# Sums and split of s4, two sums of s3 and four residual sums on VectorE instead of GpSimd

## The chip, the cores and the metric

The kernel runs on one core of a Trainium2 chip. A core has a matrix engine (PE in the profile), a vector engine (DVE), a scalar engine (ACT), a general engine (POOL, called GpSimd in the code) and a queue engine that starts transfers (SP). The metric is the device time of one execution in microseconds (us).

## The reference, cut to what matters

The kernel computes one layer of an encoder on 1024 tokens of width 1024, all in float32. Three sub-layers follow one another; each is normed ahead and behind, and added to x.

```python
def _rms_norm(x, gain):
    return x * lax.rsqrt(jnp.mean(x * x, axis=-1, keepdims=True) + RMS_EPS) * gain
def _swiglu(x, w_in, w_out):                    # w_in: 1024 x 5632, w_out: 2816 x 1024
    g, u = jnp.split(x @ w_in, 2, axis=-1)
    return (jax.nn.silu(g) * u) @ w_out
...
h = _swiglu(_rms_norm(x, ffn1_pre_norm), ffn1_w_in, ffn1_w_out)          # FFN1
x = x + 0.5 * _rms_norm(h, ffn1_post_norm)
m = _token_mixing(_rms_norm(x, mix_pre_norm), w_mix_in, ..., w_mix_out)  # mix
x = x + _rms_norm(m, mix_post_norm)
h = _swiglu(_rms_norm(x, ffn2_pre_norm), ffn2_w_in, ffn2_w_out)          # FFN2
x = x + 0.5 * _rms_norm(h, ffn2_post_norm)
```

`_token_mixing` projects to 6656 columns (`u @ w_mix_in`), runs retention and neighbourhood attention on them, and ends with the product with `w_mix_out`.

## The kernel before, in words

**Products.** PE multiplies float32 numbers as sums of shorter ones. Each operand is split in a high part and a low part: `Core.split` lets ACT cast the high part (L61) and another engine subtract it from the source to get the low part (L62). That engine is DVE unless the caller names one in `eng`. A product is then three matmuls, high with high (L88), high with low and low with high (L89, L90). A weight arrives by DMA as `wraw` and is split into `wh` and `wl` just before its use, 512 columns at a time; in the out-projection of the mix the moving operand `graw` is split in the same way into `gh` and `gl`.

**Winograd factors.** The products with the layer's input X (FFN1 and FFN2, and most of the mix's projection) use one level of the Strassen-Winograd scheme, with seven products in place of eight. `Winograd.put` makes X's seven factors, each with a high and a low half: a11, a12, a22 and the sums s1 to s4. X comes in eight token tiles of 128. For tiles 0 to 3 a call only splits a11 or a12. For tiles 4 to 7, the second half of X, a first call (g = 0) copies the transposed tile to a temporary (`cmb`, L278) and begins s3 from it (L282, L283). A second call (g = 1) splits a22 and makes s1 (L288), s2 (L290) and s4 (L293, L294); each of s1 to s4 has a split of its own (`s1h`/`s1l`, ..., `s4h`/`s4l`). `put` returns the split of s4, which the caller runs a little later. All these instructions work on 128x512 elements.

**The two transitions.** Between FFN1 and the mix (683 to 732 us in the profile), and between the mix and FFN2 (1603 to 1667 us), the tokens of one sub-layer become the factors of the next. `Core.flip` transposes a token tile on PE into the bank `pt` (L127) and calls `put` on it. In the second transition `Ep.__call__` does the end of a token first: squares and their sums on ACT (L220), `rstd` on POOL (L98, for the root of 128 numbers), the scaled row on DVE (L227), the residual sum (L229), squares again (L231), `rstd` again, and the scaled row for the next sub-layer (L118). In the kernel before, POOL makes L293, L294 and the low half of s4 for tiles 4 to 7 in both transitions; L282 and L283 for tiles 4 and 5 in the second one (`wx.s3_on_pool = (4, 5)`); and L229 for tiles 6 and 7.

**What sets the order.** Each engine works through its own list of instructions, one after the other, and waits at an instruction until what it needs is there. The lists are not in the order of the source: the framework's scheduler builds them from the whole program with a model of costs, and a change of an instruction's engine can move others. To fill PE during a transition the first products of the next sub-layer that need only a11 and a12 run between the flips. `Pairs` and `leads` do this: each begins the products of a weight tile into banks, which are finished, or added up by DVE (L509 to L535), when the other factors are there. POOL also issues the stores (L68), SP the loads.

Of the kernel before, what the change touches and what calls it, by code (L numbers as in the profile page):

```python
# [13 lines left out]
ALU = mybir.AluOpType  # L14
# [24 lines left out]
class Core:  # L39
# [6 lines left out]
    def __init__(self, tc, const, wpool, psum, dram):  # L46
        self.tc, self.nc = tc, tc.nc
        self.const, self.wpool, self.psum, self.dram = const, wpool, psum, dram
        nc = self.nc
        self.ident = const.tile([P, P], F32, name="ident")  # L50
        make_identity(nc, self.ident)
        self.mhalf = const.tile([P, 8], F32, name="mhalf")
        nc.gpsimd.memset(self.mhalf, -0.5)
        self.small = None
# [46 lines left out]
    def norm_T(self, x, gain, t, pool, put, ss=None):  # L101

        nc = self.nc
        xn = pool.tile([P, D], F32, tag="tmp", name="tmp", bufs=3)
        if ss is None:
            ss = self.small.tile([P, 3], F32, tag="ss3", name="ss3", bufs=6)
            for b in range(2):  # L110
                bs = slice(b * 512, (b + 1) * 512)
                nc.scalar.activation(xn[:, bs], x[:, bs], AF.Square, scale=1.0 / 32.0, accum_out=ss[:, b:b + 1])
        with self.tc.high_priority(offset=100):
            nc.vector.tensor_scalar(ss[:, 2:3], ss[:, 0:1], ss[:, 1:2], EPS, ALU.add, ALU.add)
            r = self.rstd(ss[:, 2:3], 1)
        for b in range(2):
            bs = slice(b * 512, (b + 1) * 512)
            nc.vector.scalar_tensor_tensor(xn[:, bs], x[:, bs], r[:, 0:1], gain[:, bs], op0=ALU.mult, op1=ALU.mult)  # L118

        return lambda: self.flip([xn[:, :512], xn[:, 512:]], t, put)  # L120

    def flip(self, halves, t, put, tag="pt", bufs=2):

        for g, h in enumerate(halves):
            pt = self.bank(tag, bufs)
            for j in range(4):
                self.nc.tensor.transpose(pt[:, j * P:(j + 1) * P], h[:, j * P:(j + 1) * P], self.ident)  # L127
            f = put(t, g, pt.rearrange("p (k t) -> p k t", k=4))
        return f
# [41 lines left out]
class Filler:  # L171
# [13 lines left out]
    def __call__(self, n):  # L185
        for _ in range(n):
            if not self.step():
                return
# [10 lines left out]
class Ep:  # L199
# [12 lines left out]
    def __call__(self, t, banks):  # L212
        c, nc = self.c, self.c.nc
        y = self.pool.tile([P, D], F32, tag="tmp", name="tmp", bufs=3)
        x = self.pool.tile([P, D], F32, tag="epx", name="epx", bufs=2)
        nc.sync.dma_start(x, self.resid(t))
        ss = c.small.tile([P, 3], F32, tag="ss3", name="ss3", bufs=6)
        f = 4.0 if self.half else 1.0
        for b in range(2):
            nc.scalar.activation(y[:, b * 512:(b + 1) * 512], banks[b], AF.Square,  # L220
                                 scale=(1.0 / 16.0 if self.half else 1.0 / 32.0), accum_out=ss[:, b:b + 1])
        nc.vector.tensor_scalar(ss[:, 2:3], ss[:, 0:1], ss[:, 1:2], f * EPS, ALU.add, ALU.add)
        r = c.rstd(ss[:, 2:3], 1)
        sx = c.small.tile([P, 3], F32, tag="ss3", name="ss3", bufs=6)
        for b in range(2):
            bs = slice(b * 512, (b + 1) * 512)
            nc.vector.scalar_tensor_tensor(y[:, bs], banks[b], r[:, 0:1], self.post[:, bs],  # L227
                                           op0=ALU.mult, op1=ALU.mult)
            (nc.gpsimd if t > 5 else nc.vector).tensor_tensor(x[:, bs], y[:, bs], x[:, bs], ALU.add)  # L229
            if self.pre is not None:  # L230
                nc.scalar.activation(y[:, bs], x[:, bs], AF.Square, scale=1.0 / 32.0, accum_out=sx[:, b:b + 1])  # L231
        (nc.sync.dma_start if self.pre is None else c.store)(self.dst(t), x)
        if self.pre is not None:
            return c.norm_T(x, self.pre, t, self.pool, self.put, sx)


class Winograd:
# [5 lines left out]

    def __init__(self, c, pools, tmp, bufs, spill=None, order=None):

        self.c, self.tmp, self.spill, self.s3_on_pool = c, tmp, spill, ()
        self.ops = {}
        if order is not None:
            for n in order:
                self.ops[n] = [pools.tile([P, 4, 512], F32R, name=f"{n}{q}") for q in "hl"]  # L250
            return
        self.pools, self.bufs = dict(zip(self.NAMES, (pools[i] for i in (0, 0, 1, 2, 2, 2, 2)))), bufs
# [10 lines left out]
    def put(self, t, g, pt):  # L263
        c, nc = self.c, self.c.nc
        ts = slice((t % 4) * P, (t % 4 + 1) * P)
        if t < 4:
            c.split(*self.part(("a11", "a12")[g], ts), pt)
            return

        def tmp():  # L270
            return self.tmp.tile([P, 4, P], F32, tag="cmb", name="cmb", bufs=4)

        h1, l1 = [q.bitcast(F32) for q in self.part("a11", ts)]
        h2, l2 = [q.bitcast(F32) for q in self.part("a12", ts)]

        if g == 0:
            self.a21, self.s3 = tmp(), tmp()
            nc.scalar.copy(self.a21, pt)  # L278
            if self.spill is not None:
                c.store(self.spill[:, :, ts], self.a21)  # L280
            eng = nc.gpsimd if t in self.s3_on_pool else nc.vector
            eng.tensor_tensor(self.s3, h1, self.a21, ALU.subtract)  # L282
            eng.tensor_tensor(self.s3, self.s3, l1, ALU.add)  # L283
            return
        a21, s3 = self.a21, self.s3
        s1 = a21 if self.spill is None else tmp()
        c.split(*self.part("a22", ts), pt)
        nc.vector.tensor_tensor(s1, pt, a21, ALU.add)  # L288
        c.split(*self.part("s3", ts), s3)
        nc.vector.tensor_tensor(s3, pt, s3, ALU.subtract)  # L290
        c.split(*self.part("s1", ts), s1)
        c.split(*self.part("s2", ts), s3)
        nc.gpsimd.tensor_tensor(s3, h2, s3, ALU.subtract)  # L293
        nc.gpsimd.tensor_tensor(s3, s3, l2, ALU.add)  # L294
        return lambda: c.split(*self.part("s4", ts), s3, eng=nc.gpsimd)


def first_factors(c, wx, pool, gpool, halves, sums, small, x, xt, gain, amid):
# [900 lines left out]
def trunk_layer(ctx: ExitStack, tc, x, xt, g1a, w1i, w1o, g1b, gma, wmt, wnv, wrv, logits, dtab, rope, bias,  # L1199
                wro, wno, wmo, gmb, g2a, w2i, w2o, g2b, out):  # L1200
    nc = tc.nc
# [5 lines left out]
    c = Core(tc, const, wpool, psum, dram)  # L1207
# [27 lines left out]
    wx = Winograd(c, apool, early, None, order=("s4", "a22", "s3", "a12", "s1", "s2", "a11"))  # L1235
# [23 lines left out]
    wx = Winograd(c, (x0pool, x1pool, spool), None, (4, 4, 2, 8, 8, 8, 8), d["a21"])  # L1259
# [224 lines left out]
    apool = pool(a_stack, "a2", "right")  # L1484
    cmb = pool(left, "cmb2")
    wx = Winograd(c, apool, cmb, None, order=("s4", "a22", "s1", "s3", "a12", "s2", "a11"))
    wx.s3_on_pool = (4, 5)
    with tc.tile_pool(name="ep2", bufs=1, reuse_waits="tile") as ep:
        rest = c.out_proj(KT, stream(c, gs, lambda k: d["m"][k]), lambda k: c.load_w(wmo[k]),
                          Ep(c, ep, gmb, g2a, False, rows(x1), rows(x2), wx.put))  # L1490
# [102 lines left out]
```

## Time and profile before

| | before |
|---|---|
| median of 3 runs | 2280.56 us (2280.09 to 2283.82) |
| profiled execution | 2281.11 us, span of its instructions 2279.3 us |
| busy share of the span | PE 97%, DVE 73%, ACT 44%, POOL 28% |
| first transition, 683 to 732 us | PE busy 40.4 of 49.0 us, DVE 43.6, ACT 23.7, POOL 24.7 |
| second transition, 1602.8 to 1667 us | PE busy 51.2 of 64.2 us, DVE 58.6, ACT 34.9, POOL 35.8 |

The profile comes from one execution. Its rows give the start of an instruction in us from the start of the span, its duration, engine, line, output and inputs; a mark such as `[1.79 <-DVE tmp L118]` says that the engine had been idle for 1.79 us and that DVE's instruction at L118 ended the wait. An instruction's duration overlaps the next one's start on its engine by a little, so the work of an engine is counted by starts. PE's clock can be lowered by the chip; the profile shows the clock that was granted as a share of full speed.

### The profile page before, as it was taken

Reading aid. Unit: us, or ns where it says so; the run is one execution under the profiler, and the core shown is the slowest. Engines: PE = TensorE matmul, PEld = TensorE weight load, DVE = VectorE, ACT = ScalarE, POOL = GpSimd, SP = SyncE. Lnnn points to the kernel's source line nnn. Section 1 sums busy time; section 2 is a strip of 40 time slices with the busy share of each in tenths; the row PEclk is TensorE's granted clock in tenths of the full one; section 3 lists DMA queues with packets and bytes.
Section 4 is the critical chain, followed back from the end, with each engine's and each line's share of the span. In section 5 each row is a group of like instructions: output and inputs, shape, how many; then the busy total and the mean of one; then the engine's idle time right before and its main releaser. Section 6 shows DMA issues by size and latency. Waiting matters only on the chain. (4 is left out here: it accounts for less than half of the span.)

```text
span 2279.3 us, 30175 instructions
## 1 busy us (share of the span) xinstructions
PE 2209.3 (97%) x10232; PEld 1830.4 (80%) x10232; DVE 1662.9 (73%) x2928; ACT 1000.5 (44%) x2086; POOL 629.9 (28%) x779
## 2 busy tenths in 40 slices
PE   7899999999998999999999999999899999999998
PEld 5678888888786887878888888887678888888886
DVE  7898878755568657769876678537988787876444
ACT  5444434332344222349875665315644343433232
POOL 1121212168424122301101222101522121115942
PEclk9999999999999999999999999999999999999999
DMA  6354434598654564557745566866535444449865
GB/s 249 134 184 145 175 130 175 197 378 293 201 178 157 176 184 128 150 174 256 218 165 165 166 217 235 292 215 208 169 134 177 161 156 158 143 146 368 304 225 181
DMA packets 152650, 448.31 MB, mean 197 GB/s; under 512 B 19312, under 2 KB 47088, under 8 KB 150384
## 3 DMA queue, kind: packets, MB, share of 16 engines
q1 hardware_dynamic: 111216, 314.23, 41.1%
q0 software_dynamic: 41280, 132.15, 16.0%
q8 instruction: 81, 1.33, 0.2%
q14 instruction: 73, 0.60, 0.1%
HBM read 305.80 MB, written 144.70 MB: 198 GB/s over the span
## 5 line engine op out<-in xcount | busy, mean ns | idle before, releaser
L62 DVE TENSOR_TENSOR wl<-wraw,wh 128x512 fp32r<-128x512 f32 x512 | 353.3, 708 | 85.4 <-ACT wh L61 84.7
L61 ACT CAST wh<-wraw 128x512 fp32r<-128x512 f32 x516 | 297.6, 618 | 192.1 <-PE ps L89 63.2
L88 PE MATMUL ps<-wh,g 128*128 128x512 f32 x484 | 188.6, 390 | 0.0
L89 PE MATMUL ps<-wl,g 128*128 128x512 f32 x484 | 188.5, 390 | 0.0
L90 PE MATMUL ps<-wh,g 128*128 128x512 f32 x484 | 188.4, 389 | 0.0
L552 ACT ACTIVATE c<-c 128x512 f32<-128x512 f32 x88 | 55.5, 632 | 204.3 <-DVE c L517 103.9
L62 DVE TENSOR_TENSOR wl<-w,wh 128x512 fp32r<-128x512 f32 x77 | 76.4, 1005 | 84.2 <-ACT wh L61 83.2
L62 DVE TENSOR_TENSOR wl<-x,wh 128x512 fp32r<-128x512 f32 x77 | 78.8, 1040 | 76.5 <-ACT wh L61 75.1
L88 PE MATMUL ps<-a11h,wh 128*128 128x512 f32 x276 | 111.6, 404 | 9.2 <-ACT wh L61 9.2
L61 ACT CAST wh<-t 128x512 fp32r<-128x512 f32 x58 | 36.0, 621 | 184.2 <-DVE t L511 184.2
L90 PE MATMUL ps<-a11h,wl 128*128 128x512 f32 x276 | 109.4, 397 | 2.6 <-DVE wl L62 2.4
L88 PE MATMUL ps<-a22h,wh 128*128 128x512 f32 x280 | 109.8, 392 | 0.0
L90 PE MATMUL ps<-a22h,wl 128*128 128x512 f32 x280 | 109.2, 390 | 0.6 <-DVE wl L62 0.6
L89 PE MATMUL ps<-a11l,wh 128*128 128x512 f32 x276 | 109.5, 397 | 0.1
L89 PE MATMUL ps<-a22l,wh 128*128 128x512 f32 x280 | 109.1, 390 | 0.0
L88 PE MATMUL ps<-a12h,wh 128*128 128x512 f32 x276 | 108.8, 394 | 0.3 <-ACT wh L61 0.3
L90 PE MATMUL ps<-a12h,wl 128*128 128x512 f32 x276 | 107.5, 390 | 0.0
L89 PE MATMUL ps<-a12l,wh 128*128 128x512 f32 x276 | 107.5, 389 | 0.0
L89 PEld LDWEIGHTS ps<-wl,g 128*128 128x128 f32 x484 | 90.9, 188 | 19.1 <-DVE wl L62 0.5
L90 PEld LDWEIGHTS ps<-wh,g 128*128 128x128 f32 x484 | 90.8, 188 | 19.0
L88 PEld LDWEIGHTS ps<-wh,g 128*128 128x128 f32 x484 | 90.9, 188 | 18.7
L88 PE MATMUL ps<-s2h,wh 128*128 128x512 f32 x232 | 91.8, 396 | 6.8 <-ACT wh L61 6.8
(433 smaller groups left out, 6443.8 us busy)
## 6 DMA issues: line engine op xcount, KB each, us to landing
wraw<-in_dram SPq DMA_DIRECT2D x218, 512.0 KB, 4.5
g<-g0s SPq DMA_DIRECT2D x44, 512.0 KB, 4.2
g<-g1s SPq DMA_DIRECT2D x44, 512.0 KB, 4.6
g<-g0a SPq DMA_DIRECT2D x33, 512.0 KB, 3.3
g<-g1a SPq DMA_DIRECT2D x33, 512.0 KB, 4.4
g0s<-gth POOLq DMA_DIRECT2D x44, 256.0 KB, 5.2
g0s<-cmb POOLq DMA_DIRECT2D x44, 256.0 KB, 3.7
g1s<-gth POOLq DMA_DIRECT2D x44, 256.0 KB, 4.9
```

What stands on the lines that cost most here:

```text
L61: self.done = [nc.scalar.copy(h, src).ins, (eng or nc.vector).tensor_tensor(l, src, hf, ALU.subtract).ins]
L62: (eng or nc.vector).tensor_tensor(l, src, hf, ALU.subtract).ins]
L88: mm(ps, a[0], b[0], start=start, stop=False)
L89: mm(ps, a[0], b[1], start=False, stop=False)
L90: mm(ps, a[1], b[0], start=False, stop=stop)
L552: nc.scalar.activation(gate[j], gate[j], AF.Silu)
```

## The change

All work of the second halves of X goes to DVE, and the three places that name POOL are gone: L293, L294 and the split of s4 (8 instructions of each, four tokens in each of two transitions), L282 and L283 for tiles 4 and 5 in the second transition (2 of each), and the residual sum L229 for tiles 6 and 7 (4). These are 32 instructions on 128x512 elements: 12 in the first transition and 20 in the second. What is computed stays the same. The rest of POOL's work (`rstd`, the issue of stores, the sums inside the FFNs) stays where it is.

```diff
@@ Ep.__call__
-            (nc.gpsimd if t > 5 else nc.vector).tensor_tensor(x[:, bs], y[:, bs], x[:, bs], ALU.add)
+            nc.vector.tensor_tensor(x[:, bs], y[:, bs], x[:, bs], ALU.add)
@@ Winograd.__init__
-        self.c, self.tmp, self.spill, self.s3_on_pool = c, tmp, spill, ()
+        self.c, self.tmp, self.spill = c, tmp, spill
@@ Winograd.put
-            eng = nc.gpsimd if t in self.s3_on_pool else nc.vector
-            eng.tensor_tensor(self.s3, h1, self.a21, ALU.subtract)
-            eng.tensor_tensor(self.s3, self.s3, l1, ALU.add)
+            nc.vector.tensor_tensor(self.s3, h1, self.a21, ALU.subtract)
+            nc.vector.tensor_tensor(self.s3, self.s3, l1, ALU.add)
...
-        nc.gpsimd.tensor_tensor(s3, h2, s3, ALU.subtract)
-        nc.gpsimd.tensor_tensor(s3, s3, l2, ALU.add)
-        return lambda: c.split(*self.part("s4", ts), s3, eng=nc.gpsimd)
+        nc.vector.tensor_tensor(s3, h2, s3, ALU.subtract)
+        nc.vector.tensor_tensor(s3, s3, l2, ALU.add)
+        return lambda: c.split(*self.part("s4", ts), s3)
@@ trunk_layer, second transition
-    wx.s3_on_pool = (4, 5)
```

One line fewer stands in `put`, so that L282, L283, L288 and L290 of the kernel before are L281, L282, L287 and L289 of the changed one, and its L293 and L294 become L292 and L293. The scheduler also builds other lists. Three places matter. The numbers behind the names tell tiles apart.

The first place is DVE's list in the first transition around the sums of token tile 7 (`cmb_6031`; `cmb_5946` is token tile 6). `wl_6071`, `wl_6088`, `wl_6107` and `wl_6124` are low halves of weights for the first products of the mix's projection. Before:

```order
L62 TENSOR_TENSOR s3l_5811<-cmb_5946,s3h_5810 128x4x128
L62 TENSOR_TENSOR wl_6071<-wraw_6067,wh_6070 128x512
L290 TENSOR_TENSOR cmb_5946<-pt_5951,cmb_5946 128x512
L62 TENSOR_TENSOR s1l_5816<-cmb_5956,s1h_5815 128x4x128
L62 TENSOR_TENSOR wl_6088<-wraw_6067,wh_6087 128x512
L62 TENSOR_TENSOR s2l_5820<-cmb_5946,s2h_5819 128x4x128
L62 TENSOR_TENSOR wl_6107<-wraw_6103,wh_6106 128x512
L62 TENSOR_TENSOR wl_6124<-wraw_6103,wh_6123 128x512
L282 TENSOR_TENSOR cmb_6031<-a11h_5217,cmb_6030 128x512
```

and with the change:

```order
L282 TENSOR_TENSOR cmb_6031<-cmb_6031,a11l_5218 128x512
L293 TENSOR_TENSOR cmb_5946<-cmb_5946,a12l_5227 128x512
L62 TENSOR_TENSOR a22l_5806<-pt_6036,a22h_5805 128x4x128
L287 TENSOR_TENSOR cmb_6041<-pt_6036,cmb_6030 128x512
L62 TENSOR_TENSOR s4l_5832<-cmb_5946,s4h_5831 128x4x128
L62 TENSOR_TENSOR s3l_5811<-cmb_6031,s3h_5810 128x4x128
L62 TENSOR_TENSOR s1l_5816<-cmb_6041,s1h_5815 128x4x128
L289 TENSOR_TENSOR cmb_6031<-pt_6036,cmb_6031 128x512
L62 TENSOR_TENSOR wl_6071<-wraw_6067,wh_6070 128x512
L62 TENSOR_TENSOR wl_6088<-wraw_6067,wh_6087 128x512
```

The low halves of these weights stood among token 6's instructions, and now they stand behind token 7's, while PE's list still has their products behind the transposes of token 7.

The second place is the end of the second transition on ACT. `s4h_14806` is the high half of s4 (of token 6 from `cmb_15951`, of token 7 from `cmb_16022`), and `wh_16156` is the weight of the first product with s3. The bracket names the engine or queue whose event a row waits for. Before:

```order
L61 CAST s3h_14812<-cmb_16022 128x4x128 [waits DVE_49]
L61 CAST s4h_14806<-cmb_15951 128x4x128 [waits Pool_49]
L61 CAST s1h_14810<-cmb_16021 128x4x128 [waits DVE_49]
L61 CAST s2h_14816<-cmb_16022 128x4x128 [waits DVE_49]
L552 ACT_TABLE_LOAD
L552 ACTIVATE c0_16123<-c0_16123 128x512 [waits DVE_49]
L61 CAST s4h_14806<-cmb_16022 128x4x128 [waits Pool_49]
L61 CAST wh_16156<-wraw_16128 128x512 [waits DMAHW6_49,DVE_49]
```

and with the change:

```order
L61 CAST s1h_14810<-cmb_16021 128x4x128 [waits DVE_49]
L61 CAST s4h_14806<-cmb_15951 128x4x128 [waits DVE_49]
L508 COPY gt_16353<-ps_16083 128x512 [waits PE_49,Activation_49]
L61 CAST s2h_14816<-cmb_16022 128x4x128 [waits DVE_49]
L61 CAST wh_16135<-t2_16130 128x512 [waits DVE_49]
L61 CAST s4h_14806<-cmb_16022 128x4x128 [waits DVE_49]
L551 ACT_TABLE_LOAD
L551 ACTIVATE c0_16123<-c0_16123 128x512 [waits DVE_49]
L61 CAST wh_16156<-wraw_16128 128x512 [waits DMAHW6_49,DVE_49]
```

Both casts of s4 now wait for DVE, and `wh_16156` still stands behind the last of them.

The third place is DVE's list in the second transition around `wl_16102`, the low half of a weight for the early products of FFN2 (`epx_15846` and `rstd_15864` belong to token 6's row for the next sub-layer, `cmb_15951` to token 6's sums and `cmb_16022` to token 7's). Before:

```order
L62 TENSOR_TENSOR wl_16064<-wraw_16043,wh_16063 128x512
L62 TENSOR_TENSOR wl_16085<-wraw_16081,wh_16084 128x512
L114 TENSOR_SCALAR ss3_15854<-ss3_15854 128x1
L62 TENSOR_TENSOR wl_16102<-wraw_16081,wh_16101 128x512
L118 SCALAR_TENSOR_TENSOR tmp_15862<-epx_15846,rstd_15864,gpre_14825 128x512 x2
```

and with the change:

```order
L62 TENSOR_TENSOR s1l_14811<-cmb_16021,s1h_14810 128x4x128
L289 TENSOR_TENSOR cmb_16022<-pt_16026,cmb_16022 128x512
L62 TENSOR_TENSOR s4l_14807<-cmb_15951,s4h_14806 128x4x128
L62 TENSOR_TENSOR wl_16102<-wraw_16081,wh_16101 128x512
L62 TENSOR_TENSOR s2l_14817<-cmb_16022,s2h_14816 128x4x128
```

It stood ahead of the rows and sums of the last two tokens, and now follows most of them.

SP's list changes in one place: the four loads of `tab` (the table for the rotary positions, L1344) stand ahead of two loads of `wraw` that they followed.

## The prediction

> **What bounds the kernel now.** I read the page first, for the busy shares, then the busy times of the two stretches that the change touches, and then PE's waits in each. In the windows the columns are length, PE, PEld, DVE, ACT and POOL busy, and the granted clock.
>
> ```profile
> PE 2209.3 (97%) x10232; PEld 1830.4 (80%) x10232; DVE 1662.9 (73%) x2928; ACT 1000.5 (44%) x2086; POOL 629.9 (28%) x779
> ```
> ```profile
> 1602.80:1667.00 64.20, 51.24 (x205) 37.82 (x204) 58.59 (x81) 34.86 (x74) 35.83 (x28) 0.92 0.36 120
> 683.00:732.00 49.00, 40.35 (x179) 31.87 (x177) 43.60 (x59) 23.65 (x44) 24.74 (x22) 0.96 0.49 160
> ```
> ```profile
> PE ps L89 <- DVE wl L62: 4.8, 3, 3.1
> PE pt L127 <- DVE tmp L118: 2.4, 2, 1.8
> PE ps L88 <- ACT wh L61: 1.8, 1, 1.8
> ```
> ```profile
> PE ps L88 <- ACT wh L61: 4.5, 1, 4.5
> PE ps L88 <- DVE ev L520: 3.0, 1, 3.0
> PE pt L127 <- DVE cmb L290: 1.5, 2, 1.2
> ```
>
> Over the whole span PE bounds the time. In the second transition PE is idle for 13 of 64.2 us and DVE for 5.6: there DVE sets the end, and PE waits mostly for its results (the first three waits). In the first transition (the last three) the 4.5 us wait is for a weight's arrival and is ahead of all that moves; the others hang on DVE.
>
> **What DVE's time consists of.** Two of the groups that move, as POOL does them, over the whole span (busy, mean ns, idle before and its cause):
>
> ```profile
> L62 POOL TENSOR_TENSOR s4l<-cmb,s4h 128x512 fp32r<-128x512 f32 x8 | 10.9, 1367 | 4.5 <-ACT s4h L61 4.4
> L229 POOL TENSOR_TENSOR epx<-tmp,epx 128x512 f32<-128x512 f32 x4 | 6.0, 1509 | 1.8 <-DVE tmp L227 1.8
> ```
>
> And what DVE does beside it, by group in the second transition, with ACT's casts of s4 there:
>
> ```profile
> L62 DVE TENSOR_TENSOR wl<-wraw,wh 128x512 fp32r<-128x512 f32 x22 | 19.3, 914 | 1.9 <-ACT wh L61 1.7
> L62 DVE TENSOR_TENSOR gl<-graw,gh 128x256 fp32r<-128x256 f32 x5 | 5.3, 1067 | 0.0
> L62 DVE TENSOR_TENSOR s1l<-cmb,s1h 128x512 fp32r<-128x512 f32 x4 | 3.9, 975 | 1.8 <-ACT s1h L61 1.8
> L229 DVE TENSOR_TENSOR epx<-tmp,epx 128x512 f32<-128x512 f32 x2 | 2.8, 1458 | 0.0
> L282 DVE TENSOR_TENSOR cmb<-a11h,cmb 128x512 f32<-128x512 f32 x2 | 2.0, 1006 | 0.0
> L283 DVE TENSOR_TENSOR cmb<-cmb,a11l 128x512 f32<-128x512 f32 x2 | 1.9, 934 | 0.0
> L530 DVE TENSOR_TENSOR wraw<-wraw,t 128x512 f32<-128x512 f32 x1 | 1.8, 1775 | 0.0
> ```
> ```profile
> L61 ACT CAST s4h<-cmb 128x512 fp32r<-128x512 f32 x4 | 2.5, 620 | 11.9 <-POOL cmb L294 11.9
> ```
>
> The single rows show why the means differ. The first fence is POOL's timeline, the second DVE's.
>
> ```profile
> 1602.14 1.30 POOL L282 TENSOR_TENSOR cmb<-a11h,cmb 128x512 f32<-128x512 f32 x1 [0.66 <-ACT cmb L278]
> 1603.52 1.61 POOL L283 TENSOR_TENSOR cmb<-cmb,a11l 128x512 f32<-128x512 f32 x1
> ```
> ```profile
> 688.92 0.68 DVE L62 TENSOR_TENSOR s3l<-cmb,s3h 128x512 fp32r<-128x512 f32 x1
> ...
> 1602.85 2.84 DVE L229 TENSOR_TENSOR epx<-tmp,epx 128x512 f32<-128x512 f32 x2
> 1605.60 0.68 DVE L62 TENSOR_TENSOR a22l<-pt,a22h 128x512 fp32r<-128x512 f32 x1
> 1606.20 0.68 DVE L288 TENSOR_TENSOR cmb<-pt,cmb 128x512 f32<-128x512 f32 x1
> ...
> 1621.48 0.41 DVE L62 TENSOR_TENSOR gl<-graw,gh 128x256 fp32r<-128x256 f32 x1
> ...
> 1656.70 1.37 DVE L62 TENSOR_TENSOR s1l<-cmb,s1h 128x512 fp32r<-128x512 f32 x1 [1.75 <-ACT s1h L61]
> ...
> 1663.91 3.16 DVE L62 TENSOR_TENSOR wl<-wraw,wh 128x512 fp32r<-128x512 f32 x4 [1.74 <-ACT wh L61]
> ```
>
> A DVE instruction on 128x512 takes 0.68 and lets the next start after 0.60 (1605.60 to 1606.20). The pair of L229 took 2.84 instead of 1.28 while POOL's two sums ran. So a DVE sum of two operands in SBUF is stretched by a POOL sum beside it: its own 0.68 grows by about the 0.6 to 1.0 of POOL's that is left.
>
> **The second transition.** DVE gets 20 instructions: 4 x 3 for s4, 4 for s3 and 4 for L229. At 0.60 each that is +12.0 us.
>
> Against it stands the stretch, which should go with POOL's sums; what POOL keeps here is `rstd` on 128 numbers and the issue of stores. By the groups: `wl` 22 x (0.914 - 0.68) = 5.1; `gl` 5 x (1.067 - 0.41) = 3.3; `s1l` 4 x 0.295 = 1.2; L229 2 x 0.78 = 1.6; L282 and L283 2 x 0.33 + 2 x 0.25 = 1.2; L530 1.1. Together -13.5.
>
> Then DVE's idle time of 5.6 us (64.20 - 58.59). Two gaps, 1.75 and 1.74, end with casts that stood in ACT's list behind `s4h`, and ACT waits 11.9 us in this window for POOL's L294. With DVE making that sum just ahead, 3.5 should go; the new wait of ACT for DVE is hidden, since between L293 and the split of s4 DVE has two other instructions (1.2 us) for one cast of 0.62. Of the other 2.1 (waits for `rstd` and small casts) I take half, since a longer list has more often something ready. Idle: -4.5; bounds 0 and -5.6.
>
> The sum for this stretch: 12.0 - 13.5 - 4.5 = -6.0, with bounds -1.5 (no idle time back) and -7.1 (all of it). These are DVE's; PE follows only if none of its own waits grows, which is a rival below.
>
> **The first transition.** The 12 instructions here are the sums and splits of s4. DVE's list puts `wl_6071` behind token 7's sums.
>
> ```profile
> 703.41 0.68 DVE L282 TENSOR_TENSOR cmb<-a11h,cmb 128x512 f32<-128x512 f32 x1
> ```
> ```profile
> 710.73 0.63 PE L127 MATMUL pt<-ident,q 128*128 128x128 f32 x4 [1.23 <-DVE cmb L290]
> ...
> 732.38 0.77 PE L88 MATMUL ps<-s1h,wh 128*128 128x512 f32 x1 [3.00 <-DVE ev L520]
> 732.95 0.63 PE L89 MATMUL ps<-s1l,wh 128*128 128x512 f32 x1
> 733.37 0.63 PE L90 MATMUL ps<-s1h,wl 128*128 128x512 f32 x1
> ...
> 735.42 0.39 PE L89 MATMUL ps<-s1l,wh 128*128 128x512 f32 x1
> 735.65 0.40 PE L90 MATMUL ps<-s1h,wl 128*128 128x512 f32 x1
> ```
>
> L282 of token 6 starts at 703.41 and should start near 703.0 (three more instructions ahead, one `wl` fewer, stretch gone). In the new list 23 instructions lie from there to `wl_6071`: 703.0 + 23 x 0.60 = 716.8, done at 717.5. PE transposes token 7 as soon as L289 of token 6 frees the bank, nine instructions after 703.0: at 709.1. The transposes take 0.4, 20 matmuls at 0.23 (735.42 to 735.65) follow, and then the first that needs `wl_6071`: at 714.0. So a wait of 3.5 us appears. In exchange the 3.00 before L520 goes: 41 instructions from 703.0 to it make 727.6, before PE comes there. The two waits of 1.5 for L290 stay about as long (1.6 by the same walk). Net: (3.5 + 1.6) - (3.0 + 1.5) = +0.6. Bounds: -0.9, if the 1.5 go as well; +2.8, if the three splits of s4 ahead each wait 0.73 for their cast (POOL's waited 4.4 over 8).
>
> After the 3.00 wait PE's matmuls start 0.43 apart (732.95 to 733.37); I take the new wait to cost the same, so this cancels. The Trainium skill, "TensorE: Matmul & The Clock Gate", Part 1, puts the lower clock after an idle window of about 3.4 us. The trace has it after 3.00 already. By that rule the new 3.5 would bring it and the old 3.00 would not have, so the first transition would come out at 0.6 + 1.2, an estimate with six matmuls at 0.2 more.
>
> SP's list has the four loads of `tab` ahead of the weight tile that DVE adds up next (L509, L510 in the new numbers).
>
> ```profile
> 712.22 3.08 SPq L1344 DMA_DIRECT2D tab<-in_dram  x4
> ```
> ```profile
> wraw<-in_dram SPq DMA_DIRECT2D x10, 512.0 KB, 4.1
> ```
>
> They wait for PE, as I read it for the last transposes of the same tiles (711.4 before). From there 0.8 to the issue, 3.1 for four and 4.1 for the weight make 719.4; DVE comes to it 30 instructions after 703.0, at 721. So I cost this at nothing, with a cover of 1.6 us; if that is gone, DVE's L520 and the products with s2 are late next.
>
> **The sum.** -6.0 + 0.6 = -5.4. The profiled execution took 2281.11 (span 2279.3, 1.8 around it), 0.55 above the median of 2280.56; -5.4 gives 2275.7 against its own time and 2275.2 as a median. Its own range is -1.5 + 2.8 = +1.3 to -7.1 - 0.9 = -8.0: 2272.6 to 2281.9. About 0.2%, or 4.6 us, can be told from no change.
>
> **The rivals.**
>
> *DVE's saving does not reach PE* (within 0.2%). PE has its own list. `wl_16102` was made at 1637.12:
>
> ```profile
> 1637.12 0.68 DVE L62 TENSOR_TENSOR wl<-wraw,wh 128x512 fp32r<-128x512 f32 x1
> ```
>
> and now stands behind 28 instructions that follow L118 of token 6: 28 x 0.60 = 16.8 and two waits for `rstd` of 0.5. From the same L118 PE has 8 transposes (1.5) and some 60 matmuls (13.6): 15.1. That is a wait of 2 to 3 us which PE did not have. If it and its slower matmuls are lost on top of DVE's bounds, the idle gain is not there: -1.5 + 0.6, 2279.7. For it: the row's new place. Against: the 1.8 at L118 and the 1.8 for `wh` go in exchange. Chance 0.2.
>
> *DVE becomes the bound* (slower). If the long rows are not POOL's doing (a port, a transfer, PE), the 13.5 stay: 12.0 - 4.5 = +7.5, and with +0.6, 2288.7. It decides where less than 3.5 of the 13.5 comes back (12.0 - 4.5 - 3.5 + 0.6 = 4.6). For it: DVE is busy for 91% of this stretch and gets 20 instructions; the reading rests on overlaps. Against: `s3l` at 688.92, with POOL idle, took 0.68, and rows with an operand in `pt` never grow. The Trainium skill, "Perfetto Trace Analysis", "Optimizing Scalar/DVE Operations", says that moving work off a saturated DVE, even to GpSimd, may make sense, but that these two share a read port, so that it might not help. The first half speaks against this change, the second for it; the stretched rows agree with the second. Chance 0.2.
>
> *More comes back* (faster still). The wait for L118 stands behind POOL's slow pair of L229 (1.5 each).
>
> ```profile
> 1639.06 1.82 PE L127 MATMUL pt<-ident,tmp 128*128 128x128 f32 x8 [1.79 <-DVE tmp L118]
> ```
>
> If it goes with a slow clock behind it (1.2, as six matmuls cost at 0.43), all idle time returns and the first transition gains 0.9: -7.1 - 0.9 - 1.2 = -9.2, 2271.4. Chance 0.1.
>
> **How the numbers follow.** The forecast has 0.5; of it 0.45 is faster by over 0.2% and 0.05 within it. The first rival gives 0.15 within and 0.05 slower, by +2.8 and a slow clock; the second 0.2 slower, the third 0.1 faster. So faster 0.55, same 0.2, slower 0.25. The range goes from 2271, near the third, to 2288, which takes in the part of the second where some stretch returns.
>
> **What would show it.** In the changed profile DVE's `wl` in the second transition should mean 0.68 to 0.72, ACT's 11.9 wait before `s4h` be under 3, and DVE's busy time be near 57 in about 58 us. A PE wait of some 3 us for `wl` should stand near 714 to 718, none for L520. If `wl` stays above 0.85, the reading of the stretch is wrong, and so is the sign.

## The result, and the profile after

The changed kernel takes 2278.10 us (median of 20 runs, 2272.30 to 2282.73) against 2282.18 for the kernel before on the same chips (20 runs, 2276.47 to 2285.86). The ratio is 0.9982, with a 95% interval of 0.9976 to 0.9989: 4.1 us faster, with 2.5 to 5.5 as bounds. That is 0.18%, clear of zero and just inside the 0.2% that the prediction called no change.

The profiled execution has a span of 2270.5 us, 8.8 less than before. It was at the fast end of the runs, so its span must not be read as the gain. PE executes the same 10232 matmuls in both kernels, so the start of the n-th one can be compared. Up to number 2750 (at 659 us) the changed kernel had already gained 1.4 us, where nothing was changed; from 2750 to 3250, with the first transition, 1.7; from 3250 to 7100, where nothing was changed either, 1.3; from 7100 to 7750, with the second transition, 4.3; behind that 0.1. The two transitions together gained 6.0 in this pair of executions.

The page of the changed kernel, first line, and its second transition between the same instructions of DVE (from the start of L229 of token 5 to the end of the fourth `wl` for the first s3 product) against the kernel before:

```profile
PE 2206.3 (97%) x10232; PEld 1829.7 (81%) x10232; DVE 1657.8 (73%) x2960; ACT 1000.8 (44%) x2086; POOL 581.5 (26%) x747
```
```profile
1597.94:1659.58 61.64, 52.09 (x209) 39.89 (x208) 58.00 (x101) 35.11 (x74) 6.05 (x8) 0.89 0.37 125
```
```profile
1602.80:1667.07 64.27, 51.31 (x206) 37.85 (x205) 58.66 (x81) 34.86 (x74) 35.83 (x28) 0.92 0.36 120
```

DVE does 101 instructions there instead of 81, in 58.0 us of busy time instead of 58.7. The groups say how (DVE, then ACT, in the same stretch of the changed kernel):

```profile
L62 DVE TENSOR_TENSOR wl<-wraw,wh 128x512 fp32r<-128x512 f32 x22 | 14.7, 686 | 0.0
L118 DVE SCALAR_TENSOR_TENSOR tmp<-epx,rstd,gpre 128x512 f32<-128x512 f32 x6 | 4.2, 748 | 1.4 <-POOL rstd L98 1.4
L227 DVE SCALAR_TENSOR_TENSOR tmp<-ps,rstd,gpost 128x512 f32<-128x512 f32 x5 | 3.6, 745 | 0.9 <-POOL rstd L98 0.9
L62 DVE TENSOR_TENSOR s4l<-cmb,s4h 128x512 fp32r<-128x512 f32 x4 | 2.7, 686 | 0.0
L62 DVE TENSOR_TENSOR s1l<-cmb,s1h 128x512 fp32r<-128x512 f32 x4 | 2.7, 684 | 0.6 <-ACT s1h L61 0.6
L62 DVE TENSOR_TENSOR gl<-graw,gh 128x256 fp32r<-128x256 f32 x5 | 2.1, 422 | 0.0
```
```profile
L61 ACT CAST s4h<-cmb 128x512 fp32r<-128x512 f32 x4 | 2.5, 620 | 5.5 <-DVE cmb L293 5.5
```

`wl` fell from a mean of 914 ns to 686, `gl` from 1067 to 422, and the 20 new instructions take 0.69 each. What is left of DVE's idle time is mostly the wait for `rstd`, 2.3 us. PE's waits in the two transitions of the changed kernel, in order of time:

```profile
706.36 0.50 PE L88 MATMUL ps<-a12h,wh 128*128 128x512 f32 x1 [0.27 <-ACT ev L1300]
707.91 0.50 PE L90 MATMUL ps<-a11h,wl 128*128 128x512 f32 x1 [0.39 <-DVE wl L62]
716.06 0.50 PE L90 MATMUL ps<-a11h,wl 128*128 128x512 f32 x1 [3.33 <-DVE wl L62]
...
1602.55 1.08 PE L127 MATMUL pt<-ident,tmp 128*128 128x128 f32 x4 [2.78 <-DVE tmp L118]
...
1632.05 1.38 PE L127 MATMUL pt<-ident,tmp 128*128 128x128 f32 x8 [1.34 <-DVE tmp L118]
...
1650.01 0.79 PE L90 MATMUL ps<-a12h,wl 128*128 128x512 f32 x1 [2.38 <-DVE wl L62]
```

In the first transition the wait of 3.0 for L520 and the two for L290 (1.5 together) are gone, and one of 3.3 for `wl_6071` is there. In the second the two waits at its end (1.83 and 0.66) and those for `gh` and `gl` are gone, and one of 2.4 for `wl_16102` is there. The waits for L118 did not go: they come to 4.7 in place of 2.4, the first of them where 3.06 for `wl` stood.

### The profile page after: what moved, and what is told of

It is laid out like the page before. It is cut to its first block, busy times and chain, and to the rows that moved or that the text cites. A ratio compares the mean times of both kernels' runs of the same rounds, so it can differ in the third digit from the quotient of the medians.

```text
span 2270.5 us, 30175 instructions
## 1 busy us (share of the span) xinstructions
PE 2206.3 (97%) x10232; PEld 1829.7 (81%) x10232; DVE 1657.8 (73%) x2960; ACT 1000.8 (44%) x2086; POOL 581.5 (26%) x747
## 5 line engine op out<-in xcount | busy, mean ns | idle before, releaser
L62 DVE TENSOR_TENSOR wl<-wraw,wh 128x512 fp32r<-128x512 f32 x512 | 344.1, 690 | 78.8 <-ACT wh L61 78.5
```

The lines of the kernel that those rows point to most:

```text
L62: (eng or nc.vector).tensor_tensor(l, src, hf, ALU.subtract).ins]
```

## The experiments

Each kernel was compared with the kernel before on the same chip; the ratio and its interval are to that. The table has, from one execution each, the two stretches in which the transitions lie (from PE's matmul 2750 to 3250, and 7100 to 7750), with PE's waits in them. Two executions of kernels with the same lists differ by up to 1.8 us in such a stretch, so single differences below that say little; several kernels share a list, and then their mean is used. In the first stretch most of this scatter goes with PE's clock, which falls to half of full speed there for one period of 3.41 us or for two, the second of which costs 1.3 to 1.8 us.

| kernel | ratio to before | first stretch, waits | second stretch, waits |
|---|---|---|---|
| before | 1 | 123.1, 9.0 | 164.6, 14.0 |
| changed | 0.9982 (0.9976 to 0.9989) | 121.4, 8.1 | 160.3, 10.5 |
| first transition only | 1.0003 (0.9989 to 1.0017) | 122.7, 8.0 | 166.3, 14.1 |
| second transition only | 0.9980 (0.9968 to 0.9992) | 123.0, 8.6 | 162.1, 13.5 |
| idle sums on POOL | 1.0055 (1.0041 to 1.0070) | 130.2, 13.3 | 170.2, 19.6 |
| s4 only | 0.9981 (0.9970 to 0.9992) | 121.4, 8.1 | 163.2, 12.5 |
| s3 and L229 only | 0.9985 (0.9975 to 0.9995) | 122.4, 8.2 | 164.7, 12.9 |
| early weights first, both | 0.9967 (0.9955 to 0.9980) | 117.7, 4.9 | 164.5, 13.5 |
| early weights first, first transition | 0.9963 (0.9951 to 0.9976) | 119.5, 5.1 | 161.3, 10.7 |
| the same, s4 later | 0.9957 (0.9944 to 0.9970) | 119.4, 5.1 | 159.2, 9.8 |

### Each transition alone

```diff
-        nc.gpsimd.tensor_tensor(s3, h2, s3, ALU.subtract)
-        nc.gpsimd.tensor_tensor(s3, s3, l2, ALU.add)
-        return lambda: c.split(*self.part("s4", ts), s3, eng=nc.gpsimd)
+        eng = nc.gpsimd if self.spill is None else nc.vector
+        eng.tensor_tensor(s3, h2, s3, ALU.subtract)
+        eng.tensor_tensor(s3, s3, l2, ALU.add)
+        return lambda: c.split(*self.part("s4", ts), s3, eng=eng)
```

Only `put` in the first transition has a spill tile, so this edit of the kernel before moves s4 in the first transition alone. The second kernel is the changed one with the opposite condition.

> Only the first transition is changed: the sums and splits of s4 go to DVE there, and the second transition keeps POOL's. Theory (each transition gives its own part, and the profile of the changed kernel shows them: 1.7 us in the first, 4.3 in the second): the time falls by 1 to 2.5 us, and PE has the new wait of about 3.3 us for wl near 716 us with none for L520. Rival (the gain is all in the second transition; what the first shows is chance between two executions): the time stays within 0.7 us of the kernel before. By the walk of the prediction it would be 0.6 us slower.

> Only the second transition is changed: s4, s3 and L229 go to DVE there, and the first transition keeps POOL's sums of s4. Theory: 4 to 5 us faster than before, DVE's wl in this stage at 0.68 to 0.72 a piece, and a PE wait of 2 to 2.5 us for a wl late in the stage. Rival (the first transition's new order also sets what the second finds): under 2 us.

The first transition alone gives a ratio of 1.0003, no change within 0.14%. The new wait is there as in the changed kernel, and the one for L520 is not:

```profile
715.67 0.50 PE L90 MATMUL ps<-a11h,wl 128*128 128x512 f32 x1 [3.35 <-DVE wl L62]
```

The three kernels with the old list of the first transition have a first stretch of 122.8 on average (123.1, 123.0, 122.4), the three with the new one 121.8 (121.4, 122.7, 121.4). PE's waits are 8.6 and 8.1. But with the old list PE's clock was halved for two periods in all three executions, and with the new one for two only in that of 122.7. At the same clock the lists come out even, so the first transition gives between nothing and 1 us. The time alone does not exclude the expected 1 to 2.5, since its interval reaches 2.5 us faster; the stretches speak for the rival.

The second transition alone gives 0.9980, 4.6 us (1.8 to 7.3), as much as the whole change. The expected wait of 2 to 2.5 for `wl` is 2.38, and its `wl` has the short form:

```profile
L62 DVE TENSOR_TENSOR wl<-wraw,wh 128x512 fp32r<-128x512 f32 x22 | 14.6, 682 | 0.0
```

The second stretch is 165.4 on average with the old list (164.6 and 166.3) and 161.2 with the new one (160.3, 162.1 and 161.3): 4.2 us.

### Idle sums on POOL

```diff
+        self.scr = const.tile([P, 512], F32, name="scr")
+
+    def extra(self, pair):
+        a, b = [q.bitcast(F32) for q in pair]
+        scr = self.scr.rearrange("p (k t) -> p k t", k=4)
+        self.nc.gpsimd.tensor_tensor(scr, a, b, ALU.add)
...
         c.split(*self.part("s3", ts), s3)
+        c.extra(self.part("s3", ts))
```

The same line follows the splits of s1 and s2. Everything that the changed kernel computes stays on the engine where it was, and the lists of PE, DVE and ACT in both transitions are the changed kernel's. SBUF, in what follows, is the memory in which the tiles lie; `pt` and `ps` are not in it but are banks that PE writes.

> The changed kernel with idle sums put on POOL: after each split of s1, s2 and s3 of tiles 4 to 7 POOL adds the two halves (128x512, both operands in SBUF) into a scratch tile that nobody reads. DVE's and PE's work is what it was. Theory (a POOL sum blocks DVE instructions with two operands in SBUF): DVE's wl, s1l, s2l and L229 in the second transition grow to 0.85 or more on average, those with an operand in pt stay at 0.68; 12 sums at about 0.7 us of stretch make the second transition 4 to 9 us longer, the first 2 to 6, the time 5 to 14 us longer than the changed kernel's. Rival (the long rows came from transfers, PE or the order of DVE's list): no DVE row grows, and the time stays within 1.5 us.

The time rose from 0.9982 to 1.0055 of the kernel before, 16.7 us, with nothing more to do for DVE or PE; 5 to 14 was expected. The first stretch grew by 8.4 us over the mean of its list (2 to 6 expected) and the second by 8.9 (4 to 9); part of the first is the clock, which was low there for four periods. In the second transition (DVE's groups; L301 is the first sum of s4, L296 the sum of s2, L235 the residual sum):

```profile
L301 DVE TENSOR_TENSOR cmb<-a12h,cmb 128x512 f32<-128x512 f32 x4 | 6.7, 1682 | 0.0
L68 DVE TENSOR_TENSOR s2l<-cmb,s2h 128x512 fp32r<-128x512 f32 x4 | 5.9, 1464 | 0.1
L235 DVE TENSOR_TENSOR epx<-tmp,epx 128x512 f32<-128x512 f32 x6 | 3.9, 683 | 0.0
L296 DVE TENSOR_TENSOR cmb<-pt,cmb 128x512 f32<-128x512 f32 x4 | 2.7, 681 | 0.0
```

The single rows show one of them (POOL's, then DVE's):

```profile
1620.53 1.33 POOL L60 TENSOR_TENSOR scr<-s2h,s2l 128x512 f32<-128x512 f32 x1 [0.69 <-DVE s2l L68]
```
```profile
1620.31 0.41 DVE L68 TENSOR_TENSOR gl<-graw,gh 128x256 fp32r<-128x256 f32 x1
1620.64 1.76 DVE L301 TENSOR_TENSOR cmb<-a12h,cmb 128x512 f32<-128x512 f32 x1
```

Of the rows that the expectation named, `s2l` and `s1l` (0.93) grew. The residual sums did not, because no idle sum ran beside them, and `wl` hardly did (0.74): one of them met an idle sum that was already running, and took 1.74. L301, which the expectation did not name, and `s2l` went from 0.69 to 1.68 and 1.46: the DVE instruction in the rows above begins 0.11 after POOL's sum and ends 0.54 after its end (1622.40 and 1621.86), about as long as its own work takes. So it is in the whole trace. DVE's sums on 128x512 that began within a POOL sum of that size (0.06 or more before its end) are 131: the 103 with both operands in SBUF all ended 0.54 to 0.61 after it, and the 28 that read `pt` or `ps` took 0.67 to 0.69. The cause of the long rows is thereby shown: a DVE sum with two operands in SBUF waits out a POOL sum that began before it. The reverse holds too: POOL's sum of that size takes 1.29 on its own, and 1.66 on average (at most 1.81) where it begins within such a DVE sum. The Trainium skill, "SBUF — State Buffer", "Who interferes with whom", says that a DVE instruction with two inputs in SBUF contends with a GpSimd instruction that reads SBUF, through a port pair that the two share as an exclusive lock, that issue order decides who blocks, and that a DVE instruction with at most one input in SBUF stays free of it. This trace agrees on all three, with the numbers above.

### s4 alone, and the rest alone

The first kernel is the kernel before with `nc.vector` in place of `nc.gpsimd` for L293, L294 and the split of s4. The second is the changed kernel with `nc.gpsimd` for these three.

> Only the sums and splits of s4 go to DVE, in both transitions; POOL keeps L282 and L283 for tiles 4 and 5 and L229 for tiles 6 and 7 in the second. Theory (the gain of the second transition comes with ACT, whose casts of s4 no longer wait for POOL, ahead of the weights' casts): the second transition is 2.5 to 4.5 us shorter than before, and the wait of 1.8 us of PE for wh at its end is gone. Rival (it comes with the residual sums, on which the transposes of tokens 6 and 7 wait): it is shorter by less than 1.5 us, and the wait for L118 near its middle is still 1.8.

> Only L282 and L283 for tiles 4 and 5 and L229 for tiles 6 and 7 go to DVE, in the second transition; POOL keeps s4. The counterpart of the kernel before it. Theory (s4): the second transition is shorter by less than 1.5 us, and PE still waits 1.5 to 2 us for wh near its end. Rival (the residual sums): 2.5 to 4.5 us shorter.

The times are 0.9981 and 0.9985, the same within their intervals, and neither is told from the whole change. Each took another wait of PE away. With s4 on DVE the 1.8 for `wh` at the end is gone and the one for L118 stays; with the residual sums on DVE it is the other way round, and four smaller waits for `wl` (0.73 to 0.88) stand ahead of it. The rows, of the first and of the second kernel:

```profile
1638.73 0.66 PE L127 MATMUL pt<-ident,tmp 128*128 128x128 f32 x4 [2.46 <-DVE tmp L118]
```
```profile
1660.64 0.50 PE L88 MATMUL ps<-s3h,wh 128*128 128x512 f32 x1 [1.45 <-ACT wh L61]
```

So both theories were too exclusive. In the stretches the second transition is 2.2 and 0.7 shorter than the mean of the old list, against 4.2 for all; with 1.8 between executions of one list this does not settle how the gain is shared.

### The new waits: a matter of order?

```diff
             for j, a in enumerate(("a11", "a12")):
                 self.begun[i].append(self.c.bank())
-                b = self.c.piece(g[:, j * 512:(j + 1) * 512])
+                with self.c.tc.high_priority(offset=40):
+                    b = self.c.piece(g[:, j * 512:(j + 1) * 512])
```

This edit of the changed kernel is in `Pairs.leads`, for the first transition, and the second kernel has it alone. The first kernel has besides it the same with 60 around the split for a12 in `Pairs.lead` of the second transition.

> The changed kernel with a higher priority in the scheduler for the splits of the early products' weights: in the first transition wl_6071 and its three neighbours stand 7 to 11 places earlier in DVE's list, in the second wl_16102 8 places earlier. Theory (the two new PE waits of 3.3 and 2.4 us are only a matter of order): both waits go below 1 us, and the time is 2.5 to 5 us below the changed kernel's. Rival (DVE's whole work sets the end of both stages): as much wait turns up at the next product or transpose, and the time is within 1 us of the changed kernel's.

> The changed kernel with the higher priority for the early products' weights in the first transition alone; the second transition's list is the changed kernel's. Theory (in the first transition the wait for wl is a matter of order, in the second DVE's whole work sets the end, so that there the priority only moved the wait to the next product): the first transition is 3 to 4 us shorter than the changed kernel's, the second as long as its, the time 2.5 to 4.5 us below it and 6 to 9 below the kernel before. Rival (the priority in the second transition helped as well): slower than the kernel that has both by 1.5 us or more.

In the first transition the wait of 3.3 vanished and none came in its place; three kernels with these splits early have PE waits of 4.9 to 5.1 there instead of 8.1, and a first stretch of 118.9 on average instead of 121.8. At the same clock the gain is 3.3 with two slow periods (119.4 and 119.5 against 122.7) and 3.7 with one (117.7 against 121.4), about the wait that went. In the second transition the 2.4 for `wl_16102` vanished too, and 3.6 us of wait turned up at the product with s2:

```profile
1653.59 0.50 PE L88 MATMUL ps<-s2h,wh 128*128 128x512 f32 x1 [2.54 <-ACT wh L61]
1655.34 0.80 PE L90 MATMUL ps<-s2h,wl 128*128 128x512 f32 x1 [1.02 <-DVE wl L62]
```

The cast that ends the first is that of t2, a sum of weights for this product (L510 of the changed kernel), which stands in DVE's list behind token 6's sums of s4. So the first theory holds for the first transition and the rival for the second. Without the priority in the second transition its stretch is the changed kernel's again (161.3). The times, 0.9967 and 0.9963, do not tell these two apart.

### s4 later

The kernel before it (early weights first in the first transition), with this edit:

```diff
-        nc.vector.tensor_tensor(s3, h2, s3, ALU.subtract)
-        nc.vector.tensor_tensor(s3, s3, l2, ALU.add)
-        return lambda: c.split(*self.part("s4", ts), s3)
+        def late():
+            with c.tc.high_priority(offset=-40):
+                nc.vector.tensor_tensor(s3, h2, s3, ALU.subtract)
+                nc.vector.tensor_tensor(s3, s3, l2, ALU.add)
+                c.split(*self.part("s4", ts), s3)
+        return late
```

> As the kernel before it, and the sums and splits of s4 get a lower priority: in the second transition those of tokens 6 and 7 stand behind the sums that the first product with s2 needs (t2 and its low half), and two more splits of weights move ahead of them. The product with s4 is the last of its group. Theory (at the end of the second transition PE waits for what stands behind s4 in DVE's list): the wait of 2.4 us for wl and what follows it falls to 1 us or less, the second transition is 1.5 to 3.5 us shorter than the changed kernel's, and this is the fastest of all. Rival (the sums of s4 then hold up later work by as much): the second transition is within 1 us of the changed kernel's.

The wait of 2.4 became one of 0.4 at an early product and one of 0.4 at the product with s2:

```profile
1644.01 0.50 PE L90 MATMUL ps<-a11h,wl 128*128 128x512 f32 x1 [0.38 <-DVE wl L62]
1650.02 0.50 PE L90 MATMUL ps<-s2h,wl 128*128 128x512 f32 x1 [0.42 <-DVE wl L62]
```

The second stretch is 159.2, 2.0 below the mean of the changed list, which is what was expected, but from one execution. PE's waits there are 9.8, against 10.5 to 13.5 with that list. The time is 2271.73 us (6 runs, 2269.41 to 2272.97), a ratio of 0.9957 (0.9944 to 0.9970): some 10 us below the kernel before, and the lowest median. It beats both kernels; that it beats the one before it (0.9963) is not shown.

## Why the prediction was right, and where its sum was not

The time (2278.1 in 2271 to 2288) and the sign came as forecast. The predicted gain of 5.4 was 4.1. That the two are so close is partly luck: DVE's list gave back less than half of what was forecast for it, and PE gained more than that list did. By its own terms:

- **The stretch: right.** Predicted 13.5 us for the second transition. DVE's busy time there went from 58.66 to 58.00 with 20 x 0.60 = 12.0 added: 12.7 came back. `wl` gave 22 x (0.914 - 0.686) = 5.0 of the 5.1. The second rival, that the long rows are not POOL's doing, fell with this and with the idle sums.
- **DVE's idle time: the term that was mis-sized.** "Idle: -4.5" measured -2.0: from 64.27 - 58.66 = 5.6 to 61.64 - 58.00 = 3.6. The step that failed is "Of the other 2.1 ... I take half". The two gaps behind `s4h` did go, but the waits for `rstd` before L118 and L227 grew from 1.0 + 0.4 to 1.4 + 0.9, the one for ACT before L114 from 0.2 to 0.7, and one of 0.6 for `s1h` came. The longer list did not fill the waits for `rstd`: in both lists a single DVE instruction stands between the one that `rstd` needs (L114 or L222) and the row that waits for it. So DVE's busy time, told as near 57 in about 58 us, was 58.0 in 61.6. That ACT's wait ahead of `s4h` would be under 3 was also wrong: it was 5.5, but `s4l` behind it shows no idle time of DVE.
- **The second transition's sum.** Predicted -6.0; DVE's list became 2.6 shorter between the same instructions, and PE's stretch 4.2 (in the same pair of executions 4.3, of which 0.4 lies ahead of the transition and 0.4 behind). So PE did not follow DVE's list one for one. Its two last waits (1.83 and 0.66) were for a cast and a split at the end of this list, and with the change these came in time. How PE's surplus divides among its waits was not separated.
- **The first transition.** Predicted +0.6, measured 0 to -1.0, and about 0 at the same clock. The new wait for `wl_6071`, 3.5 by the walk, is 3.33. The 3.00 for L520 went as told. The two for L290, kept at 1.6, went: 0.27 and 0.39 are all that is there.
- **The clock.** "I take the new wait to cost the same" was wrong in this execution and right in another. Behind the 3.33 PE ran at full speed, while behind the 3.00 of the kernel before it had not, nor behind the 3.35 of the kernel with the first transition alone, whose list there is the same. The clock is the third number from the end (712 to 722 us of the changed kernel, 730 to 740 of the kernel before, 712 to 722 of the first transition only):

```profile
712.00:722.00 10.00, 6.67 (x30) 5.17 (x29) 10.00 (x18) 2.31 (x4) 0.56 (x1) 1.00 0.29 106
```
```profile
730.00:740.00 10.00, 7.62 (x28) 6.21 (x29) 8.40 (x14) 3.35 (x7) 0.66 (x2) 0.83 0.38 131
```
```profile
712.00:722.00 10.00, 6.65 (x23) 5.07 (x22) 10.00 (x18) 2.26 (x5) 0.56 (x1) 0.83 0.32 115
```

- **The first rival** had its mechanism: the wait for `wl_16102` is 2.38 where 2 to 3 was told. What it lacked is that the waits that go in exchange were larger: all of PE's waits in the stretch fell from 14.0 to 10.5. The 1.8 at L118, named against it, stayed in good part (1.34). It put the gain at 0.9, the forecast at 5.4; the measured 4.1 lies between the two, nearer to the forecast.
- **The loads of `tab`**, costed at nothing, show no wait that could be put down to them.

## What to carry to other kernels

Moving an elementwise sum from DVE to POOL frees DVE only where what DVE runs meanwhile reads at most one operand from SBUF; here each POOL sum cost DVE about as much as doing it (12.7 us for 20 of them, against 12.0). To see it, compare the mean of one group of rows beside POOL's work and away from it. And where a busy engine gets more work, look at what the scheduler pushes behind it: with the order mended the same change gave 7.5 to 10 us in place of 4. Whether the kernel before would gain from the same priorities was not tried.

## What the runs showed of the hardware

The price of a PE wait is not fixed. The same wait of 2.38 us occurs at 867 us of the changed kernel and at 866 us of the kernel with early weights first in the first transition alone, outside all that was changed. In the first PE's clock was lowered afterwards, and PE came 1.45 us later to the same matmul; in the second it was not (windows of 860 to 870 us, the granted clock third from the end):

```profile
860.00:870.00 10.00, 7.62 (x30) 5.94 (x29) 8.94 (x15) 1.49 (x3) 5.30 (x8) 0.90 0.66 118
```
```profile
860.00:870.00 10.00, 7.62 (x33) 5.76 (x33) 8.96 (x14) 2.30 (x5) 5.21 (x7) 1.00 0.69 130
```

The length of this part of the program (matmuls 3250 to 4250) was 229.5 in six of the ten executions and 231.0 in the other four, and nothing between. The ten traces show what decides it. In each of them the times at which the granted clock falls to half lie whole multiples of 3.413 us apart, and it stays there for one to three such periods. So time can be cut into periods of 3.413 us, and PE's idle time counted in each. Between 60 and 2255 us, 60 periods at full clock hold at least 1.87 us of it, and behind 59 of them the clock is halved; of the 2608 with less, that holds behind 3. The border of 1.87 is read from these same traces, and PE's idle time rests on modelled ends. The 2.38 of the changed kernel fell into one period, that of the other kernel into two (PE idle for 0.86 and 1.52 in them); the 3.33 of the first transition fell into two (1.71 and 1.62), while 2.51 of the 3.00 of the kernel before fell into one.

The Trainium skill, "TensorE: Matmul & The Clock Gate", Part 1, says that the window is free-running, about 3.4 us long, and does not reset when a kernel starts. The traces agree on the length, and the grid lies differently to the program's start from trace to trace. Its table puts the lower clock after an idle window of about 3.4 us; the trace has it after a wait of 2.38.
